# The low part of the weights, made by an adding DMA in one granule of eight of the feed-forward products

## The chip, the cores and the metric

The kernel runs on one core of a Trainium2 chip. The metric is the device time of one execution in microseconds (us): the median over the runs, before and after the change. The core has five engines that work side by side and meet at semaphores: TensorE (matmuls, PE in the profile), VectorE (DVE), ScalarE (ACT), GpSimd (POOL) and SyncE (SP, which here only issues DMAs). Data lies in SBUF, matmuls add up in PSUM, and DMAs move data between HBM and SBUF.

## The reference

One layer of a decoder trunk in float32, for 256 tokens of width 2048. Cut to what matters:

```python
h = rms_norm(x, norm_mix)
proj = h @ w_in                       # 2048 x 5400, for four mixers
...                                   # the mixers; each normed; concatenated
x = x + mixed @ w_out                 # 2048 x 2048
h = rms_norm(x, norm_ffn)
x = x + (silu(h @ w_ffn_gate) * (h @ w_ffn_up)) @ w_ffn_down
#            2048 x 5632           2048 x 5632       5632 x 2048
```

The feed-forward part, the last line, is what the change touches.

## The kernel before, in words

Every large product goes through the generator `product` (L120). It multiplies both tiles of 128 tokens by one block of 512 columns of a weight matrix, and so has two accumulators in PSUM, `a[0]` and `a[1]`. Weights and activations are split in two parts each, a rounded high part and the low part that is left, and three of the four partial products are summed: high by high (L146), high by the weights' low part (L147), low by the weights' high part (L148).

The rows of the weight matrix are taken in granules of two blocks of 128 (GRAN = 2). For each granule:

- SyncE loads 512 KB into `raw` (L134; six buffers of 128 partitions by 1024 floats),
- ScalarE copies it rounded into `wh` (L137; three buffers),
- VectorE makes `wl`, `raw` minus `wh` (L138; three buffers),
- TensorE runs 12 matmuls: two token tiles by two blocks by L146, L147, L148.

The feed-forward part (L785 to L805) runs, for each of 11 blocks of 512 hidden columns, a gate product and an up product of 8 granules each. ScalarE applies Silu to the gate's sums (L790), VectorE multiplies by the up product (L793), and `hidden_T` transposes the result and splits it into `gh` and `gl` (L777 to L782); it runs after granule 1 of the next gate product. Then come four down products of 22 granules each, one for each 512 output columns; VectorE adds the residual (L804), and SyncE and ScalarE store. That makes 11 x 8 + 11 x 8 + 4 x 22 = 264 granules.

The program is written in order, but a scheduler lays down the order of each engine's instructions when the program is built (L836, `TileContext` with a timeline simulation): it may put an instruction ahead of another one when the other's inputs or buffers are, in its model, not yet there. On the chip each engine then runs its own list in that order, and waits on semaphores for data and for buffers to come free.

Of the kernel before, what the change touches and what calls it, by code (L numbers as in the profile page):

```python
# [8 lines left out]
F32 = mybir.dt.float32  # L9
F32R = mybir.dt.float32r  # L10
BF16 = mybir.dt.bfloat16
AF = mybir.ActivationFunctionType
ALU = mybir.AluOpType
# [4 lines left out]
P = 128  # L18
T = 256
D_MODEL = 2048  # L20
KT = D_MODEL // P
# [12 lines left out]

# First distance of each relative-position bucket (distances up to T - 1).
BUCKET_STARTS = [0, 1, 2, 3, 4, 5, 6, 7, 8, 9, 10, 11, 12, 13, 14, 15, 16, 21, 27, 35, 46, 59, 77,
                 99, 128, 166, 216]

# Columns of w_in.
C_Q, C_KV, C_B, C_C, C_D = 0, 512, 1304, 2840, 3864  # L40


class Blocks:
    """A [P, KT, T] operand kept as tiles of four blocks each."""

# [9 lines left out]
def trunk(ctx: ExitStack, tc: tile.TileContext, x, w_in, w_out, norm_mix, norm_ffn, q_gain, k_gain,  # L55
# [10 lines left out]

# [1 line left out]
    nc.scalar.preload_act_table_set("natural_log_exp_and_others")  # L68
# [19 lines left out]

    # the tensor engine runs at half its clock until it has been busy for a while
    warm = misc.tile([P, GW], F32, name="ps")  # L90
# [10 lines left out]

# [1 line left out]
    def rstd(pool, ss, n, count, eps, name):  # L103
        """(ss / count + eps) ** -0.5 over [P, n]."""
        r = pool.tile([ss.shape[0], n], F32, name=name)
        nc.gpsimd.tensor_scalar(r, ss, 1.0 / count, eps, op0=ALU.mult, op1=ALU.add)
        nc.gpsimd.tensor_tensor(r, r, mhalf[:ss.shape[0], :n], op=ALU.pow)
        return r

    def split_T(hi, lo, kt, srcs, gain):  # L110
        """Transposes of two token tiles into column block kt of hi and lo, times gain."""
        p = misc.tile([P, GW], F32, name="ps")
        for t in range(2):
            nc.tensor.transpose(p[:, t * P:(t + 1) * P], srcs[t], ident)  # L114
        g = gain[:, kt:kt + 1]
        nc.scalar.activation(hi[:, kt, :], p[:, :T], AF.Copy, scale=g)  # L116
        nc.vector.scalar_tensor_tensor(lo[:, kt, :], p[:, :T], g, hi[:, kt, :].bitcast(F32),
                                       op0=ALU.mult, op1=ALU.subtract)

    def product(w, c0, n, hi, lo, nkt, order=None, before=None, mids=()):  # L120
        """[hi + lo]^T @ w[:, c0:c0 + n] for both token tiles, in three passes of 12-bit parts.

        Yields after each granule of GRAN blocks; mids[i] runs after granule i + 1."""
        a = [acc.tile([P, GW], F32, name="acc") for _ in range(2)]
        order = list(order or range(0, nkt, GRAN))
        for g, k0 in enumerate(order):
# [5 lines left out]
            for i in range(0, GRAN, step):  # L132
                ii = slice(i, i + step)
                nc.sync.dma_start(raw[:, ii, :n], wv[:, ii, :])  # L134
                if before is not None and i == 0:
                    before(k0)
                nc.scalar.activation(wh[:, ii, :n], raw[:, ii, :n], AF.Copy)  # L137
                nc.vector.tensor_tensor(wl[:, ii, :n], raw[:, ii, :n], wh[:, ii, :n].bitcast(F32),  # L138
                                        op=ALU.subtract)
# [16 lines left out]
    def residual(c, a):  # L156
        """Add a to column chunk c of x, and take its sum of squares."""
        for t in range(2):
# [5 lines left out]
    def run(gen):  # L164
        """Drive a generator to its end."""
        while True:
            try:
                next(gen)
            except StopIteration as e:
                return e.value  # L170

# [1 line left out]
    h1h = hpool.tile([P, KT, T], F32R, name="h1h", tag="hh")  # L173
# [25 lines left out]
    def slot(k, name, shape=(P, 2, GW), dtype=F32):  # L199
        """One of the eight tiles that end up holding the mixed operand."""  # L200
        return mp.tile(list(shape), dtype, name=name, tag=f"m{k}")
# [5 lines left out]
    with tc.tile_pool(name="mix", bufs=1) as mix:  # L207
# [18 lines left out]
        def group_norm(o):  # L226
            """RMSNorm, without the gain, of o [P, 2, GW] in place."""
            s = mix.tile([P, 2], F32, name="gss", bufs=2)
# [7 lines left out]
        def group_T(o, group, k):  # L236
            """o, transposed and times the gain, as a group's blocks of the mixed operand."""
            mixed(group, k)
            for kt in range(4):
                split_T(mh, ml, group * 4 + kt, [o[:, t, kt * P:(kt + 1) * P] for t in range(2)], ggain)  # L240

# [1 line left out]
        oh = mix.tile([32, 256], F32, name="oh", tag="quarter", bufs=2)  # L243
# [13 lines left out]

        # ================= group A: native sparse attention ======================================
        # ---- queries
        qs = evacuate(aq, "qs", dst=slot(2, "qs"))  # L260
# [41 lines left out]

        # ---- compressed branch
        zp = slot(1, "zp", (P, 16, 2, 2, NCMP))
# [17 lines left out]

        # ---- keys, values, gates
        w1 = [slot(4 + b, f"w1_{b}", (P, 8, 2, 64)) for b in range(2)]
# [8 lines left out]
        a = run(product(w_in, C_KV, 512, h1h, h1l, KT, mids=[None, None, None, queries_T]))  # L333
        # the compressed branch's columns twice over, for a transpose into both halves
        for t in range(2):
# [7 lines left out]

        # ---- the other products, a granule at a time between the steps of the attention
        mids, got = {}, {}
# [104 lines left out]

        # gates: wg[p, r, g, t, b] = sigmoid
        ge = mix.tile([P, 2, 24], F32, name="ge")
# [6 lines left out]

        # masks  # L460
        negf = mix.tile([P, P], F32, name="negf", tag="quarter", bufs=2)
# [21 lines left out]
        nc.gpsimd.memset(hc, 0.0)  # L483
        # gelu(h) = h / (1 + exp(-2 c (h + 0.044715 h^3)))
        h_ = mix.tile([P, 2 * NCMP], F32, name="h_")
# [12 lines left out]
        pump(1)  # L498
        # keys: kcT[(g', d), (g, n)], zero where g' != g
        p = misc.tile([P, GW], F32, name="ps")  # L500
# [15 lines left out]
        nc.scalar.activation(kcT, p[:, :32], AF.Copy, scale=gk)  # L516
        # values: vcb[(r, g, n), (r', g'), d], zero off the diagonal
        hv = mix.tile([P, 4, 32], F32, name="hv", tag="quarter", bufs=2)
# [7 lines left out]
        pump(1)  # L526
        # scores and softmax
        rv = const.tile([P, 2], F32, name="rv")
# [37 lines left out]

        # ---- selected (all blocks are) and window (all keys are in reach) branches
        mn = mix.tile([P, 4, 2, 2, 2], F32, name="mn")
# [68 lines left out]

        # ================= group D: stick-breaking attention ======================================
        od = big("od")
        zs, ss, parts, ats = {}, {}, {}, {}  # L640

        def diagonal(v):
            """Zero the query-key pairs of the diagonal blocks whose key isn't before the query."""
            v = v.rearrange("p (b c) -> p b c", c=P)[:, 0:3:2, :]
# [3 lines left out]
        def logits(h):  # L648
# [5 lines left out]
                             skip_group_check=True)  # L654
            # softplus(z) = max(z, 0) + log(1 + exp(-|z|))
            b = mix.tile([P, 384], F32, name="e", bufs=3)
# [52 lines left out]
        group_T(od, 3, 2)  # L709
        # ================= group C: causal spatial gating =========================================  # L710
        tril = const.tile([P, P], F32, name="tril")
# [30 lines left out]

        # both wait with group C's blocks until it is done
        outs = [out_product(0, [spatial]), out_product(1, [lambda: group_T(uu, 2, 6)])]
# [5 lines left out]

    # ================= output projection, residual, transposed FFN input ==========================
    h2h = hpool.tile([P, KT, T], F32R, name="h2h", tag="hh")
# [13 lines left out]
    with tc.tile_pool(name="ffn", bufs=2) as ffn:  # L766
        # ================= SwiGLU FFN =============================================================
        gh = ffn.tile([P, FKT, T], F32R, name="gh", bufs=1)
# [16 lines left out]
        for c in range(NFF):  # L785
            before_ = (lambda: input_T(3)) if c == 0 else (lambda: hidden_T(c - 1))
            a = run(product(w_gate, c * GW, GW, h2h, h2l, KT, mids=[before_]))
            s = ups[c] = ffn.tile([P, 2, GW], F32, name="s")
            for t in range(2):
                nc.scalar.activation(s[:, t, :], a[t], AF.Silu, scale=rs2[:, t:t + 1])  # L790
            a = run(product(w_up, c * GW, GW, h2h, h2l, KT))
            for t in range(2):
# [3 lines left out]
        for c in range(4):  # L796
            a = run(product(w_down, c * GW, GW, gh, gl, FKT,
                            mids=[lambda: hidden_T(NFF - 1)] if c == 0 else ()))
# [41 lines left out]
```

## Time and profile before

| | |
|---|---|
| median of 2 runs | 1142.0 us (1141.68 to 1142.32) |
| span of the profiled execution | 1141.3 us |
| TensorE busy, share of the span | 99% |
| VectorE busy | 51% |
| ScalarE busy | 46% |
| GpSimd busy | 5% |
| moved by DMA | 208.85 MB, mean 183 GB/s |

The profile is of one execution, taken by the hardware profiler. Its span runs from the first to the last instruction and here lies 0.7 us below the median of the timed runs. Its views: a page with the busy time of each engine, the chain of work that ended last (followed back from the last instruction to what released it, step by step), the costliest groups of instructions and the DMA issues; the waits, by who waited for whom; the timeline of single instructions; and tables of busy time by stretch, with the clock granted to TensorE (1.00 is full) and the busy share of the 16 DMA engines. In these views L and a number is a line of the kernel, `out<-in` names the tiles, and PEld is TensorE's weight load, which runs beside the matmuls. Matmuls overlap each other: one shows 0.39 us, but the next starts earlier.

### The profile page before, as it was taken

How to read it: one execution, taken by the hardware profiler on the slowest of the kernel's cores; microseconds unless marked ns; L12 is line 12 of the kernel's file. 1: busy time of each engine (PE TensorE's matmuls, PEld its weight loads, DVE VectorE, ACT ScalarE, POOL GpSimd, SP SyncE). 2: the span in 40 equal slices, each digit the busy share in tenths (PEclk: the TensorE clock that was granted, in tenths of full speed). 3: DMA queues.
4: the chain of work that ended last, by engine and by line, in shares of the span. 5: the costliest groups of instructions: out<-in, count | busy, mean ns of one | idle time of the engine just before them, and what ended most of it. 6: DMA issues, size and time to landing. Idle time of an engine off the chain costs nothing.

```text
span 1141.3 us, 13742 instructions
## 1 busy us (share of the span) xinstructions
PE 1131.6 (99%) x5275; PEld 935.9 (82%) x5275; DVE 587.0 (51%) x697; ACT 520.2 (46%) x669; POOL 54.2 (5%) x96
## 2 busy tenths in 40 slices
PE   8999999999999999999999999999999999999998
PEld 6898777888888888888888888888888888888887
DVE  5565444556566554454454554544544544444443
ACT  6454455555545544444444444444444434343432
POOL 3210001222000000000000000000000000000000
PEclk9999999999999999999999999999999999999999
DMA  9774433545555566666666666666666567666761
GB/s 279 250 259 146 146 112 111 152 144 148 165 171 177 178 190 190 186 188 196 186 186 198 187 189 189 190 190 186 189 195 186 186 197 209 199 206 197 204 199 62
DMA packets 115186, 208.85 MB, mean 183 GB/s; under 512 B 11204, under 2 KB 18464, under 8 KB 114992
## 3 DMA queue, kind: packets, MB, share of 16 engines
q1 hardware_dynamic: 113168, 204.21, 60.5%
q0 software_dynamic: 800, 2.71, 0.7%
q10 hardware_dynamic: 1152, 1.05, 0.3%
q8 instruction: 41, 0.67, 0.2%
q14 instruction: 25, 0.20, 0.1%
HBM read 205.84 MB, written 3.68 MB: 184 GB/s over the span
## 4 chain that ended last, share of the span: by engine, by line
PE 98%; DMA 1%; DVE 0%; SPq 0%; ACT 0%; issue 0%; DVEq 0%
PE acc L147 30%; PE acc L148 30%; PE acc L146 30%; PE ps L777 1%; PE ps L114 1%; DMA xs<-in_x 1%; PE ps L580 1%; PE ps L592 1%; PE ps L579 1%; PE ps L652 0%; PE ps L605 0%; PE ps L480 0%; PE ps L603 0%; DVE zp L317 0%; PE ps L604 0%; PE ps L653 0%
## 5 line engine op out<-in xcount | busy, mean ns | idle before, releaser
L138 DVE TENSOR_TENSOR wl<-raw,wh 128x1024 fp32r<-128x1024 f32 (+2 forms) x385 | 466.9, 1213 | 493.5 <-ACT wh L137 493.3
L137 ACT ACTIVATE wh<-raw 128x1024 fp32r<-128x1024 f32 (+2 forms) x385 | 404.1, 1050 | 535.1 <-PE acc L148 506.3
L148 PE MATMUL acc<-wh,h2l 128*128 128x512 f32 x704 | 274.0, 389 | 0.0
L147 PE MATMUL acc<-wl,h2h 128*128 128x512 f32 x704 | 273.9, 389 | 0.0
L146 PE MATMUL acc<-wh,h2h 128*128 128x512 f32 x704 | 249.9, 390 | 0.0
L148 PEld LDWEIGHTS acc<-wh,h2l 128*128 128x128 f32 x704 | 132.1, 188 | 27.6
L147 PEld LDWEIGHTS acc<-wl,h2h 128*128 128x128 f32 x704 | 132.2, 188 | 27.1
L146 PEld LDWEIGHTS acc<-wh,h2h 128*128 128x128 f32 x704 | 132.2, 188 | 27.1
L148 PE MATMUL acc<-wh,gl 128*128 128x512 f32 x352 | 137.0, 389 | 0.0
L147 PE MATMUL acc<-wl,gh 128*128 128x512 f32 x352 | 136.9, 389 | 0.0
L147 PE MATMUL acc<-wl,h1h 128*128 128x512 f32 (+1 forms) x352 | 136.4, 388 | 0.4 <-DVE wl L138 0.4
L146 PE MATMUL acc<-wh,h1h 128*128 128x512 f32 (+1 forms) x352 | 132.7, 391 | 1.7 <-ACT h1h L116 1.7
L148 PE MATMUL acc<-wh,h1l 128*128 128x512 f32 (+1 forms) x352 | 134.2, 388 | 0.0
L146 PE MATMUL acc<-wh,gh 128*128 128x512 f32 x352 | 123.1, 389 | 0.0
L146 PEld LDWEIGHTS acc<-wh,h1h 128*128 128x128 f32 x352 | 66.1, 189 | 14.7 <-ACT h1h L116 2.0
L147 PEld LDWEIGHTS acc<-wl,h1h 128*128 128x128 f32 x352 | 66.5, 189 | 13.4 <-issue 1.0
L146 PEld LDWEIGHTS acc<-wh,gh 128*128 128x128 f32 x352 | 66.0, 188 | 13.8
L147 PEld LDWEIGHTS acc<-wl,gh 128*128 128x128 f32 x352 | 66.1, 188 | 13.7
L148 PEld LDWEIGHTS acc<-wh,gl 128*128 128x128 f32 x352 | 66.1, 188 | 13.7
L148 PEld LDWEIGHTS acc<-wh,h1l 128*128 128x128 f32 x352 | 66.0, 189 | 12.3 <-DVE wl L138 0.4
L147 PE MATMUL acc<-wl,mh 128*128 128x512 f32 x128 | 50.1, 393 | 0.0
L148 PE MATMUL acc<-wh,ml 128*128 128x512 f32 x128 | 49.4, 391 | 0.0
(259 smaller groups left out, 654.2 us busy)
## 6 DMA issues: line engine op xcount, KB each, us to landing
raw<-in_w_ffn_gate SPq DMA_DIRECT2D x88, 512.0 KB, 4.4
raw<-in_w_ffn_up SPq DMA_DIRECT2D x88, 512.0 KB, 3.7
raw<-in_w_ffn_down SPq DMA_DIRECT2D x88, 512.0 KB, 4.5
raw<-in_w_in SPq DMA_DIRECT2D x79, 512.0 KB, 3.6
raw<-in_w_out SPq DMA_DIRECT2D x32, 512.0 KB, 3.9
raw<-in_w_in SPq DMA_DIRECT2D x8, 280.0 KB, 3.7
xs<-in_x SPq DMA_DIRECT2D x8, 256.0 KB, 8.2
cdr<-cdr POOLq DMA_DIRECT2D x1, 1536.0 KB, 9.2
```

The source lines that it names most:

```text
L114: nc.tensor.transpose(p[:, t * P:(t + 1) * P], srcs[t], ident)
L137: nc.scalar.activation(wh[:, ii, :n], raw[:, ii, :n], AF.Copy)
L138: nc.vector.tensor_tensor(wl[:, ii, :n], raw[:, ii, :n], wh[:, ii, :n].bitcast(F32), op=ALU.subtract)
L146: nc.tensor.matmul(a[t][:, :n], h, wh[:, i, :n], start=first, stop=False)
L147: nc.tensor.matmul(a[t][:, :n], h, wl[:, i, :n], start=False, stop=False)
L148: nc.tensor.matmul(a[t][:, :n], l, wh[:, i, :n], start=False, stop=last)
L579: nc.tensor.matmul(s[:, 0:128], q_[:, 0:128], k_[:, 0:128], start=True, stop=True)
L580: nc.tensor.matmul(s[:, 128:384], q_[:, 128:256], k_, start=True, stop=True)
L592: nc.tensor.transpose(p[:, c * P:(c + 1) * P], es[u][:, c * P:(c + 1) * P], ident)
L777: nc.tensor.transpose(p[:, i * T + t * P:i * T + (t + 1) * P], ups[c][:, t, (2 * k + i) * P:(2 * k + i + 1) * P], ident)
```

## The change

`product` gets a list, `dma_low`, of granules whose low part is made in another way. In such a granule ScalarE writes minus the rounded `raw` into `wl` (a second copy, with scale -1), and a DMA issued from GpSimd adds `raw` onto `wl` in SBUF; VectorE's subtract is left out. Gate and up products name granule 5 (of 0 to 7), the down products granules 5 and 13 (of 0 to 21).

```diff
-    def product(w, c0, n, hi, lo, nkt, order=None, before=None, mids=()):
+    def product(w, c0, n, hi, lo, nkt, order=None, before=None, mids=(), dma_low=()):
...
                 nc.scalar.activation(wh[:, ii, :n], raw[:, ii, :n], AF.Copy)
+                if g in dma_low:
+                    nc.scalar.activation(wl[:, ii, :n], raw[:, ii, :n], AF.Copy, scale=-1.0)
+                    nc.gpsimd.dma_start(wl[:, ii, :n].bitcast(F32), raw[:, ii, :n], accum_op=ALU.add)
+                    continue
                 nc.vector.tensor_tensor(wl[:, ii, :n], raw[:, ii, :n], wh[:, ii, :n].bitcast(F32),
                                         op=ALU.subtract)
...
-            a = run(product(w_gate, c * GW, GW, h2h, h2l, KT, mids=[before_]))
+            a = run(product(w_gate, c * GW, GW, h2h, h2l, KT, mids=[before_], dma_low=(5,)))
...
-            a = run(product(w_up, c * GW, GW, h2h, h2l, KT))
+            a = run(product(w_up, c * GW, GW, h2h, h2l, KT, dma_low=(5,)))
...
-            a = run(product(w_down, c * GW, GW, gh, gl, FKT,
+            a = run(product(w_down, c * GW, GW, gh, gl, FKT, dma_low=(5, 13),
                             mids=[lambda: hidden_T(NFF - 1)] if c == 0 else ()))
```

The rest of the diff takes comments out.

## Rows read from the trace of the kernel before

**Rows 1.** The page: busy time of each engine; the chain that ended last.

```profile
PE 1131.6 (99%) x5275; PEld 935.9 (82%) x5275; DVE 587.0 (51%) x697; ACT 520.2 (46%) x669; POOL 54.2 (5%) x96
...
PE 98%; DMA 1%; DVE 0%; SPq 0%; ACT 0%; issue 0%; DVEq 0%
```

**Rows 2.** TensorE's waits, first and last of five: us, times, longest.

```profile
PE ps L93 <- POOL ident masks.py:199: 2.6, 1, 2.6
...
PE acc L147 <- DVE wl L138: 0.4, 1, 0.4
```

**Rows 3.** The page's groups: busy us, mean ns, idle before, what ended it.

```profile
L138 DVE TENSOR_TENSOR wl<-raw,wh 128x1024 fp32r<-128x1024 f32 (+2 forms) x385 | 466.9, 1213 | 493.5 <-ACT wh L137 493.3
L137 ACT ACTIVATE wh<-raw 128x1024 fp32r<-128x1024 f32 (+2 forms) x385 | 404.1, 1050 | 535.1 <-PE acc L148 506.3
```

**Rows 4.** Timeline, 702.5 to 709 us: start, us, engine, instruction, idle before.

```profile
702.55 0.39 PE L147 MATMUL acc<-wl,h2h 128*128 128x512 f32 x1
702.78 0.39 PE L148 MATMUL acc<-wh,h2l 128*128 128x512 f32 x1
...
703.00 0.62 PE L146 MATMUL acc<-wh,h2h 128*128 128x512 f32 x2
703.20 1.06 ACT L137 ACTIVATE wh<-raw 128x1024 fp32r<-128x1024 f32 x1 [1.66 <-PE acc L148]
...
704.30 1.23 DVE L138 TENSOR_TENSOR wl<-raw,wh 128x1024 fp32r<-128x1024 f32 x1 [1.50 <-ACT wh L137]
...
708.44 0.62 PE L146 MATMUL acc<-wh,h2h 128*128 128x512 f32 x2
...
708.90 0.39 PE L147 MATMUL acc<-wl,h2h 128*128 128x512 f32 x1
```

**Rows 5.** Stretches of 510 to 1141: length, busy by engine, clock, DMA share, GB/s.

```profile
700.00:850.00 150.00, 150.00 (x675) 124.40 (x675) 74.41 (x67) 64.01 (x66) 0.00 (x0) 1.00 0.65 190
...
sum 631.00, PE 627.49 PEld 519.91 DVE 305.20 ACT 259.10 POOL 0.00; mean PE 125.50 PEld 103.98 DVE 61.04 ACT 51.82 POOL 0.00
```

**Rows 6.** Timeline of GpSimd: the issue of its 1024 KB DMA.

```profile
54.98 0.92 POOL L255 DMA_DIRECT2D tb<-cdr  x1 [8.86 <-DMA cdr<-cdr]
```

**Rows 7.** DMA issues: count, KB each, median us from issue to landing.

```profile
raw<-in_w_ffn_gate SPq DMA_DIRECT2D x88, 512.0 KB, 4.4
...
cdr<-cdr POOLq DMA_DIRECT2D x1, 1536.0 KB, 9.2
...
tb<-cdr POOLq DMA_DIRECT2D x1, 1024.0 KB, 6.7
...
cdr<-csb POOLq DMA_DIRECT2D x1, 12.0 KB, 2.6
```

**Rows 8.** The stretch of 2 us with the highest rate, 44 to 64 us.

```profile
58.00:60.00 2.00, 2.00 (x13) 1.77 (x13) 0.11 (x1) 1.67 (x4) 0.00 (x0) 1.00 1.06 392
```

**Rows 9.** Timeline of TensorE behind the pair of L146 at 703.00.

```profile
703.91 0.39 PE L146 MATMUL acc<-wh,h2h 128*128 128x512 f32 x1
704.14 0.39 PE L147 MATMUL acc<-wl,h2h 128*128 128x512 f32 x1
704.36 0.39 PE L148 MATMUL acc<-wh,h2l 128*128 128x512 f32 x1
704.59 0.39 PE L147 MATMUL acc<-wl,h2h 128*128 128x512 f32 x1
```

**Rows 10.** DMA queues: packets, MB, share of 16 engines' span; the loads' queue.

```profile
q1 hardware_dynamic: 113168, 204.21, 60.5%
```

**Rows 11.** Timeline of TensorE from 6 us; stretches of 1 us, 9 to 13 us.

```profile
8.16 0.50 PE L146 MATMUL acc<-wh,h1h 128*128 128x512 f32 x1 [1.74 <-ACT h1h L116]
...
9.93 0.47 PE L114 MATMUL ps<-ident,xs 128*128 128x128 f32 x1 [0.56 <-DMA xs<-in_x]
...
9.00:10.00 1.00, 0.44 (x3) 0.07 (x2) 0.44 (x1) 0.89 (x2) 1.00 (x6) 0.71 1.08 353
10.00:11.00 1.00, 1.00 (x5) 1.00 (x6) 1.00 (x2) 0.00 (x0) 1.00 (x2) 0.50 1.08 374
...
12.00:13.00 1.00, 1.00 (x4) 0.77 (x4) 0.39 (x1) 1.00 (x3) 0.00 (x0) 0.58 1.10 361
```

## The prediction

> **What bounds the kernel now.** I read the page first. TensorE is busy for 99% of the span, VectorE for 51%, ScalarE for 46%, GpSimd for 5%, and the chain that ended last runs through TensorE for 98% of the span [rows 1]. So the reader is to see one full engine and three with room. TensorE's waits of over 0.15 us are five in the whole run, the longest 2.6 us at the start and the shortest 0.4 us, and none of their lines belongs to the feed-forward part alone [rows 2]. VectorE's subtract (L138) is busy for 466.9 us, but VectorE has been idle for 493.5 us ahead of its instances; of ScalarE's rounding copy (L137) it is 404.1 and 535.1, mostly until TensorE gives a buffer back [rows 3]. Taking work from VectorE can therefore gain nothing: no matmul of this stage waits for it.
>
> Next the timeline of the middle of a gate product, for how far ahead the parts are made [rows 4]. A granule is 12 matmuls and begins with a pair of L146; from 703.00 to 708.44 there are two of them, so one takes 2.72 us, 12 x 0.227 us, without a gap. With three `wh` and three `wl`, the end of a granule frees buffers for the one three later: the copy that starts at 703.20 makes `wh` for the granule of 708.44. It ends at 704.26, the subtract runs from 704.30 to 705.53, and the first matmul that reads this `wl` (L147) is due at 708.90. The low part is ready 3.37 us early. That cover is all that the change can spend.
>
> **The change, part by part.** It touches granule 5 of each gate and up product, 11 + 11, and granules 5 and 13 of the four down products, 8: 30 granules of 264.
>
> *Removed:* 30 subtracts of 1.23 us, 37 us of VectorE. Worth nothing on the path, by the 3.37 us above.
>
> *Added on ScalarE:* 30 copies with scale -1, of the form of L137, 1.06 us each, 32 us. Ahead of an L137 ScalarE has been idle for 1.66 us [rows 4], and no Silu or transposed hidden block stands at these granules, so the copy doesn't delay the next `wh`. But the DMA must wait for it. In the program's order (`wh` first) it runs from 704.26 to 705.32, and GpSimd can issue at about 705.36, with the 0.04 us that VectorE needs behind ScalarE.
>
> *Added on GpSimd's queue:* 30 DMAs of 512 KB from SBUF to SBUF that add onto their destination. GpSimd does nothing in the stage [rows 5], so nothing is queued behind them. The largest issue took GpSimd 0.92 us [rows 6]; that lies within the landing times below. No row shows an accumulating DMA, nor one between SBUF tiles, so its landing is bounded by the plain ones of that queue: 12 KB took 2.6 us, 1024 KB 6.7 us, 1536 KB 9.2 us from issue to landing [rows 7], all beside weight loads.
> - Lower end: the fixed 2.6 us, and 512 KB at the best rate of a 2 us stretch, 392 GB/s [rows 8], 1.3 us: 3.9 us. As a plain copy between the 12 KB and the 1024 KB row: 2.6 + 500/1012 x 4.1 = 4.6 us.
> - Middle: an add has to read the source and the old destination, 1024 KB in: the 1024 KB row, 6.7 us.
> - Upper end: two reads and the write in turn, 1536 KB: 9.2 us.
>
> I take 6.7 us, because the second read can't be left out, while the write can run beside reads, as it did in the copies of those rows. The Trainium skill (Collectives: The Full Stack, "Why ReduceScatter is half of AllGather") says that the add in a DMA costs nothing by itself but needs two source reads on one read queue, and so halves the rate; by that the middle is right, and no run here shows it yet. The Trainium skill's fit for a DMA from this queue (DMA: Bandwidth & Descriptors, "Anatomy of one DMA") is 2.0 us plus the bytes at 436 GB/s; an estimate by it is 3.2 us for 512 KB and would leave no stall, but the same fit gives 4.4 us for the 1024 KB that took 6.7 us here, so the row decides.
>
> *The stall.* 705.36 + 6.7 = 712.06 against 708.90: 3.16 us. Can TensorE do something else meanwhile? In the order of this run the L147 at 704.59 has no L146 just ahead of it: that L146 is the second of the pair at 703.00, the first one of the other accumulator, taken ahead. Within one accumulator the order L146, L147, L148 is kept [rows 9]. So after two matmuls both accumulators stand before an L147, and the next product can't start, because its `wh` needs a buffer of the granules in between. Nothing fills the gap, and nothing gives it back, since TensorE has no idle time later. What is late next is nothing: the two granules behind have their parts ready by then, and the following copies again run two granules ahead. So 30 x 3.16 = 95 us. The profiled span of 1141.3 us lies 0.7 us below the median of 1142.0, so I add to the median: 1142 + 95 = **1237 us**.
>
> *Loads.* `raw` is held until the DMA lands, 712.06 in place of 705.53, and the load of the granule six later waits for it, with SP's later loads queued behind. That load's `wh` starts 5.24 us before its granule of 708.44 + 6 x 2.72 = 724.76, at 719.52: 14.0 us after 705.53, of which the load takes 4.4 [rows 7]. Of the 9.6 us left 6.5 go, while the granule itself moves by 3.2. Hidden; without this cover each us would come on top 30 times. The loads' queue takes 0.605 of 1141.3 us for 204.21 MB [rows 10], 1.77 us per 512 KB; two passes are 3.5 us in a product of 8 granules, 21.8 us, so that the share of 0.65 [rows 5] becomes about 0.8. That is not full.
>
> **The rivals.**
> 1. *The clock falls too, or the landing is long.* Between 6.4 and 9.9 us TensorE stood still for 1.74 us, ran four matmuls, stood for another 0.56 us, and the granted clock went to the lower level: 0.71, 0.50, 0.50, 0.58 of full in the four us from 9 to 13 [rows 11]. That lost 0.29 + 0.50 + 0.50 + 0.42 = 1.7 us. A stall of 3.2 us is longer than those two together, but has full work on both sides. If each of the 30 brings it, 51 us: 1288 us. If the landing takes 9.2 us, the stall is 5.66 us and the time 1312 us, with the clock 1363 us. For it: nothing in the rows excludes it. Against: in the feed-forward stage the clock has been 1.00 throughout [rows 5], but with no stall to test it.
> 2. *The stall is smaller.* The minus copy needs only `raw` and a `wl`, and the last reader of a `wl` (702.55 + 0.39 = 702.94) ends before the last of the `wh` (703.17). The order on each engine is laid down at build by a scheduler that moves instructions, as the L146 shows. If it puts the minus copy first, ScalarE ends it at 704.03, the issue is at 704.07, and 6.7 us leave 1.87 us: 56 us, 1198 us. Against: the program has `wh` first. A plain copy's 4.6 us in the program's order leaves 1.06 us, 32 us, 1174 us.
> 3. *Hidden: not slower.* The cover decides. With the minus copy first the DMA has 4.83 us, and a landing of 4.6 or 3.9 us fits: 1142 us. In the program's order it has 3.54 us, and 3.9 us leaves 0.36 us, 11 us in all, 1153 us, within 2%. Both need an add that costs no more than a plain copy. The Trainium skill's fit named above would make it so, and the 1024 KB row disagrees with it. A time below 1142 us has no mechanism, since 12 x 0.227 us per granule stay: a small chance only.
> 4. *It doesn't do what it says:* other matmuls might fill the stall. The three buffers exclude that, as said; it is counted under 3.
>
> **How the numbers follow.** Forecast (a stall of about 2 to 4 us in the program's order, the clock held): 0.42, its own range 1200 to 1265 us. Rival 1: 0.28, above 1265 us, up to 1363. Rival 2: 0.15, 1165 to 1200 us. Rivals 3 and 4: 0.13 within 2%, 1142 to 1165 us, and 0.02 faster. Under 2% (23 us) is about what a measurement of this kernel can't tell from no change. So faster 0.02, same 0.13, slower 0.42 + 0.28 + 0.15 = 0.85. The range leaves out rival 3 and the very longest landings: 1160 to 1360 us.
>
> **What would show each step.** In the profile of the changed kernel: 355 subtracts in place of 385; a new group of 30 copies of 1.06 us; 30 DMAs of 512 KB from GpSimd, whose median landing I expect at 6.7 us; a wait of TensorE, at the matmul that reads `wl`, for that DMA, 30 times and about 3.2 us each, 95 us in all, where there was none; a chain that ended last with some 8% of DMA and less TensorE. The order of the two copies on ScalarE tells rival 2, the granted clock behind each stall rival 1. The prediction is wrong if the landing is under 3.5 us or over 9.2 us, or if TensorE has other work in the stall.

## The result and the profile after

The changed kernel takes 1168.54 us in the median of two runs (1167.38 to 1169.69) against 1142.0 us: a ratio of 1.023, with a 95% interval of 1.0213 to 1.0247. It is slower, in the direction forecast, but by 26.5 us and not by 95 us. The profiled execution has a span of 1167.7 us, 26.4 us more than before, so the profile holds the whole of the loss.

The page of the changed kernel: busy time, the chain that ended last by engine, and the groups that answer to [rows 1] and [rows 3] (busy us, mean ns, idle before, what ended it). The numbers of lines are now five higher.

```profile
PE 1139.8 (98%) x5275; PEld 933.6 (80%) x5275; DVE 549.8 (47%) x667; ACT 548.6 (47%) x699; POOL 80.3 (7%) x126
...
PE 79%; DMA 13%; issue 3%; ACT 2%; DVE 1%; SPq 0%; DVEq 0%; POOLq 0%; ACTq 0%
...
L143 DVE TENSOR_TENSOR wl<-raw,wh 128x1024 fp32r<-128x1024 f32 (+2 forms) x355 | 429.7, 1211 | 556.0 <-ACT wh L138 554.2
...
L141 POOL DMA_DIRECT2D wl<-raw x30 | 26.0, 865 | 696.7 <-ACT wl L140 580.9
L140 ACT ACTIVATE wl<-raw 128x1024 fp32r<-128x1024 f32 x30 | 31.8, 1061 | 41.5 <-PE acc L152 41.5
...
wl<-raw POOLq DMA_DIRECT2D x30, 512.0 KB, 5.4
```

The parts are those that the diff says: 30 subtracts fewer, 30 copies of 1.06 us and 30 DMAs of 512 KB more, with a median landing of 5.4 us. VectorE has given up 37 us and nothing came of it. Two entries differ from what was expected: the landing, 5.4 in place of 6.7 us, and what ended ScalarE's idle time ahead of the minus copy. That is TensorE's L152, the last reader of a `wl`, and not the copy into `wh`.

TensorE's waits (us in total, times, longest) answer to [rows 2]:

```profile
PEld acc L152 <- DMA wl<-raw: 30.3, 30, 1.9
...
PE acc L152 <- DMA wl<-raw: 17.8, 21, 1.5
```

The first row counts from when the weight load could have run, the second only the idle time after the running matmul has ended; the loss lies between them. Counted from the timeline, as the time between when a first L152 was due and when it started, the 30 stalls sum to 22.5 us, 0.75 us in the mean, from 0.00 to 1.61 us; the matmul after a stall also takes 0.34 us to the next in place of 0.227, some 3 us more in all. That leaves about 1 us of the 26.4 us unexplained. One stall in the timeline, in the first down product (TensorE's other matmuls left out):

```profile
1007.02 1.06 ACT L140 ACTIVATE wl<-raw 128x1024 fp32r<-128x1024 f32 x1 [1.43 <-PE acc L152]
...
1007.98 1.04 ACT L138 ACTIVATE wh<-raw 128x1024 fp32r<-128x1024 f32 x1
...
1008.37 0.86 POOL L141 DMA_DIRECT2D wl<-raw  x1 [21.67 <-ACT wl L140]
...
1012.48 0.61 PE L151 MATMUL acc<-wh,gh 128*128 128x512 f32 x2
...
1014.07 0.19 PEld L152 LDWEIGHTS acc<-wl,gh 128*128 128x128 f32 x1 [1.40 <-DMA wl<-raw]
1014.07 0.50 PE L152 MATMUL acc<-wl,gh 128*128 128x512 f32 x1 [0.97 <-DMA wl<-raw]
...
1014.41 0.40 PE L153 MATMUL acc<-wh,gl 128*128 128x512 f32 x1
```

The minus copy (L140) comes first, the copy into `wh` (L138) after it. GpSimd issues 0.29 us behind the end of the copy (1008.08 to 1008.37). The pair of L151 starts at 1012.48, so L152 was due 2 x 0.227 us later, at 1012.94, and ran at 1014.07: 1.13 us late, 5.7 us after the issue. The weight load (PEld) of that L152 waits for the DMA too and starts together with the matmul, where elsewhere it runs ahead; that would explain the 0.34 us, but no run separates it. This is rival 2 of the prediction, with a shorter landing than it used.

### The profile page after: what moved, and what is told of

Its sections match the earlier page's. It is cut to its first block, busy times and chain, and to the rows that moved or that the text cites. A ratio compares the mean times of both kernels' runs of the same rounds, so it can differ in the third digit from the quotient of the medians.

```text
span 1167.7 us, 13830 instructions
## 1 busy us (share of the span) xinstructions
PE 1139.8 (98%) x5275; PEld 933.6 (80%) x5275; DVE 549.8 (47%) x667; ACT 548.6 (47%) x699; POOL 80.3 (7%) x126
## 4 chain that ended last, share of the span: by engine, by line
PE 79%; DMA 13%; issue 3%; ACT 2%; DVE 1%; SPq 0%; DVEq 0%; POOLq 0%; ACTq 0%
PE acc L152 25%; PE acc L153 24%; PE acc L151 23%; DMA wl<-raw 11%; ACT wl L140 2%; DMA raw<-in_w_ffn_down 1%; PE ps L114 1%; PE ps L782 1%; DVE wl L143 1%; ACT wh L138 1%; PE ps L585 1%; PE ps L597 1%; DMA xs<-in_x 1%; PE ps L584 1%; DMA raw<-in_w_ffn_gate 0%
## 5 line engine op out<-in xcount | busy, mean ns | idle before, releaser
L143 DVE TENSOR_TENSOR wl<-raw,wh 128x1024 fp32r<-128x1024 f32 (+2 forms) x355 | 429.7, 1211 | 556.0 <-ACT wh L138 554.2
L138 ACT ACTIVATE wh<-raw 128x1024 fp32r<-128x1024 f32 (+2 forms) x385 | 403.4, 1048 | 490.7 <-PE acc L153 470.5
L152 PE MATMUL acc<-wl,h2h 128*128 128x512 f32 x704 | 276.5, 393 | 10.4 <-DMA wl<-raw 9.9
L153 PE MATMUL acc<-wh,h2l 128*128 128x512 f32 x704 | 274.3, 390 | 0.0
L151 PE MATMUL acc<-wh,h2h 128*128 128x512 f32 x704 | 250.0, 391 | 0.0
L152 PEld LDWEIGHTS acc<-wl,h2h 128*128 128x128 f32 x704 | 132.2, 188 | 45.6 <-DMA wl<-raw 19.0
L151 PEld LDWEIGHTS acc<-wh,h2h 128*128 128x128 f32 x704 | 132.2, 188 | 27.2
L153 PEld LDWEIGHTS acc<-wh,h2l 128*128 128x128 f32 x704 | 132.2, 188 | 26.9
L152 PE MATMUL acc<-wl,gh 128*128 128x512 f32 x352 | 137.9, 392 | 7.9 <-DMA wl<-raw 7.9
L153 PE MATMUL acc<-wh,gl 128*128 128x512 f32 x352 | 137.0, 389 | 0.0
L152 PE MATMUL acc<-wl,h1h 128*128 128x512 f32 (+1 forms) x352 | 136.3, 388 | 0.4 <-DVE wl L143 0.4
L153 PE MATMUL acc<-wh,h1l 128*128 128x512 f32 (+1 forms) x352 | 134.2, 388 | 0.0
L151 PE MATMUL acc<-wh,h1h 128*128 128x512 f32 (+1 forms) x352 | 132.6, 391 | 1.5 <-ACT h1h L116 1.5
L151 PE MATMUL acc<-wh,gh 128*128 128x512 f32 x352 | 123.0, 389 | 0.0
L152 PEld LDWEIGHTS acc<-wl,gh 128*128 128x128 f32 x352 | 66.1, 188 | 24.8 <-DMA wl<-raw 11.3
L151 PEld LDWEIGHTS acc<-wh,h1h 128*128 128x128 f32 x352 | 66.1, 189 | 14.4 <-ACT h1h L116 1.8
L152 PEld LDWEIGHTS acc<-wl,h1h 128*128 128x128 f32 x352 | 66.5, 189 | 13.4 <-issue 1.0
L151 PEld LDWEIGHTS acc<-wh,gh 128*128 128x128 f32 x352 | 66.1, 188 | 13.7
L153 PEld LDWEIGHTS acc<-wh,gl 128*128 128x128 f32 x352 | 66.1, 188 | 13.5
L153 PEld LDWEIGHTS acc<-wh,h1l 128*128 128x128 f32 x352 | 66.0, 189 | 12.3 <-DVE wl L143 0.4
L141 POOL DMA_DIRECT2D wl<-raw x30 | 26.0, 865 | 696.7 <-ACT wl L140 580.9
L140 ACT ACTIVATE wl<-raw 128x1024 fp32r<-128x1024 f32 x30 | 31.8, 1061 | 41.5 <-PE acc L152 41.5
```

The source lines that it names most:

```text
L140: nc.scalar.activation(wl[:, ii, :n], raw[:, ii, :n], AF.Copy, scale=-1.0)
L141: nc.gpsimd.dma_start(wl[:, ii, :n].bitcast(F32), raw[:, ii, :n], accum_op=ALU.add)
L151: nc.tensor.matmul(a[t][:, :n], h, wh[:, i, :n], start=first, stop=False)
L152: nc.tensor.matmul(a[t][:, :n], h, wl[:, i, :n], start=False, stop=False)
L153: nc.tensor.matmul(a[t][:, :n], l, wh[:, i, :n], start=False, stop=last)
```

## The experiments

**What is to be told apart.** Theory: each stall is the DMA's landing less its cover, the time from the issue to the first L152; the cover is set by the `wl` buffer that comes free and by which copy ScalarE makes first, and the landing by the second read of the add and by the weight loads beside it. Rivals: the order of the copies is of no account; ScalarE's second copy is itself what costs; the DMA costs through the loads that it delays; the landing is fixed cost, and the add is free.

**The order of the two copies.** The minus copy is made to depend on `wh`:

```diff
-                    nc.scalar.activation(wl[:, ii, :n], raw[:, ii, :n], AF.Copy, scale=-1.0)
+                    nc.scalar.activation(wl[:, ii, :n], wh[:, ii, :n].bitcast(F32), AF.Copy, scale=-1.0)
```

> The minus copy reads wh instead of raw (the same values), so that ScalarE has to make wh first, as the program is written. Theory (the stall is the DMA's landing less the cover, and the cover is set by which copy comes first): the issue moves back by the 0.97 us from one copy's start to the next, each of the 30 stalls grows by about as much, 29 us in all, from 1168.5 to about 1197 us. Rival (the order of the copies is of no account, because something else, such as the DMA engines' load, ends the wait): 1165 to 1172 us. If stalls of some 2 us made the clock fall, over 1220 us.

Measured: 1196.03 us, ratio 1.0473 (1.0457 to 1.0488). The timeline of one granule:

```profile
513.49 1.06 ACT L138 ACTIVATE wh<-raw 128x1024 fp32r<-128x1024 f32 x1 [1.58 <-PE acc L153]
514.58 1.06 ACT L140 ACTIVATE wl<-wh 128x1024 fp32r<-128x1024 f32 x1
515.93 0.85 POOL L141 DMA_DIRECT2D wl<-raw  x1 [23.57 <-ACT wl L140]
...
518.73 0.61 PE L151 MATMUL acc<-wh,h2h 128*128 128x512 f32 x2
520.77 0.50 PE L152 MATMUL acc<-wl,h2h 128*128 128x512 f32 x1 [1.43 <-DMA wl<-raw]
```

The minus copy starts 1.09 us after the copy into `wh`, as the prediction had it, and the stall here is 520.77 - 518.73 - 0.45 = 1.59 us; 28 of the 30 lie between 1.5 and 1.7 us. So forcing the order costs 1196.0 - 1168.5 = 27.5 us, near the 29 us of the theory, but by two errors that offset each other: the issue moved back by 1.3 us (3.25 us ahead of when L152 is due, in place of 4.57) and not by 0.97 us, while the landing, 4.8 us in the median, is 0.6 us shorter than in the changed kernel, which the theory didn't have. The longest stall is 2.6 us, and the clock granted in the 2 us stretches around it stayed at 1.00:

```profile
1079.07 0.50 PE L152 MATMUL acc<-wl,gh 128*128 128x512 f32 x1 [2.44 <-DMA wl<-raw]
```

```profile
1080.00:1082.00 2.00, 2.00 (x11) 1.64 (x10) 0.00 (x0) 0.28 (x1) 0.00 (x0) 1.00 0.77 195
```

**A buffer of its own for the low part.** In the 30 granules `wl` comes from the feed-forward part's pool, one buffer:

```diff
-            wl = wpool.tile([P, GRAN, GW], F32R, name="wl")
+            if g in dma_low:
+                wl = low_pool.tile([P, GRAN, GW], F32R, name="wd", bufs=1)
+            else:
+                wl = wpool.tile([P, GRAN, GW], F32R, name="wl")
...
```

> The low part of the 30 granules gets a buffer of its own, apart from the three wl, so that the minus copy needs no release by the granule three before. Theory (the cover is short only because the wl buffer comes free 5.5 us before the first matmul that reads it): the copy and the DMA run a granule or more earlier, no stall is left, 1142 to 1145 us. Rival (the DMA costs through the DMA engines or the held raw buffer, by delaying weight loads): still over 1155 us, with TensorE or ScalarE waiting for raw.

Measured: 1143.19 us, ratio 1.0007 (0.9998 to 1.0016). TensorE has no wait for the DMA left; in one granule the minus copy waits only for `raw` and starts 16.6 us before the L155 that reads its `wd`:

```profile
494.97 1.06 ACT L143 ACTIVATE wd<-raw 128x1024 fp32r<-128x1024 f32 x1 [2.32 <-DMA raw<-in_w_ffn_gate]
...
511.55 0.39 PE L155 MATMUL acc<-wd,h2h 128*128 128x512 f32 x1
```

The same 30 DMAs, with landings of 4.7 to 6.8 us, now cost nothing that can be measured. So the loss is the short cover, and not the DMA engines' load. This run says nothing of the held `raw`: all 30 DMAs land before the copy into `wh` of the same granule starts (here at 501.12 and 508.80 us), and that copy holds `raw` as long as before. The changed kernel does: there `raw` is held until the landing, and its waits show none of TensorE or of a ScalarE copy for a load in the feed-forward part.

**The add itself.** A plain copy in place of the adding one:

```diff
-                    nc.gpsimd.dma_start(wl[:, ii, :n].bitcast(F32), raw[:, ii, :n], accum_op=ALU.add)
+                    nc.gpsimd.dma_start(wl[:, ii, :n].bitcast(F32), raw[:, ii, :n])
```

> The DMA copies raw onto wl without adding; the low part of these granules is therefore wrong (it holds the whole weight). All else is as in the changed kernel, the order of the copies too. Theory (the add costs a second read, so that 512 KB move at 197 GB/s where a plain load reaches 390): the transfer takes 1.3 to 1.5 us less, landing at about 4 us in place of 5.4, within the cover: 1142 to 1148 us. Rival (the landing is fixed cost and waiting behind the weight loads, the add is free): landing stays over 5 us, 1163 to 1170 us.

Measured: 1147.91 us, ratio 1.0047 (1.003 to 1.0063), with ScalarE's order as in the changed kernel. Landings, shortest, median and longest, in the changed kernel and here:

```profile
DMA to landing us min/median/max: 4.5/5.4/6.1
```

```profile
DMA to landing us min/median/max: 2.9/4.0/5.3
```

The add costs 1.6 us on the shortest landing and 1.4 us on the median; without it, 20.6 of the 26.5 us are gone. How long the DMA engines are taken by it stands in the pages, in the row of GpSimd's queue (packets, MB, share of 16 engines' span): before, in the changed kernel, and here.

```profile
q0 software_dynamic: 800, 2.71, 0.7%
```

```profile
q0 software_dynamic: 5120, 18.44, 7.8%
```

```profile
q0 software_dynamic: 5120, 18.44, 4.2%
```

Less the 8 us of before (0.7% of 1141.3), 30 DMAs take 83 us with the add and 40 us without: 2.8 and 1.3 us each for the same 512 KB written. The add takes the engines twice as long. That this is the second read is the reading that fits; the rows count what is written and show no read.

**VectorE in place of the DMA.** The minus copy stays:

```diff
-                    nc.gpsimd.dma_start(wl[:, ii, :n].bitcast(F32), raw[:, ii, :n], accum_op=ALU.add)
+                    nc.vector.tensor_tensor(wl[:, ii, :n], raw[:, ii, :n], wl[:, ii, :n].bitcast(F32), op=ALU.add)
```

> The minus copy stays on ScalarE, and VectorE adds raw onto it in place of the DMA. Theory (ScalarE has room, and only the DMA's landing costs): 1142 us, as before, no wait of TensorE. Rival (the extra copy of 1.06 us delays the next wh or its matmuls): up to 30 x 1.06 = 32 us more, 1160 to 1174 us.

Measured: 1142.6 us, ratio 0.9999 (0.999 to 1.0008), no wait of TensorE in the feed-forward part. ScalarE's extra copy is hidden.

**Fewer loads beside the DMA.** In the feed-forward products three of four granules use the `raw` of the one before:

```diff
-            raw = wpool.tile([P, GRAN, GW], F32, name="raw", bufs=6)
+            fresh = not dma_low or g % 4 == 0
+            if fresh:
+                raw = wpool.tile([P, GRAN, GW], F32, name="raw", bufs=6)
...
-                nc.sync.dma_start(raw[:, ii, :n], wv[:, ii, :])
+                if fresh:
+                    nc.sync.dma_start(raw[:, ii, :n], wv[:, ii, :])
```

> In the feed-forward part only every fourth granule is loaded, and the three after it use the same raw (so the products there use wrong weights); the minus copy, the DMA and all matmuls stay. Theory (the landing runs from 4.5 to 6.1 us because weight loads share the DMA engines with it): all landings come near the lowest, 4.5 us, and the stalls sum to under 6 us: 1143 to 1149 us. Rival (the spread comes from GpSimd's issue or from VectorE beside it): landings stay at 5.4 us in the median, 1163 to 1170 us.

> The same quarter of the loads, but the low part made by VectorE in every granule, as before the change: what fewer loads do to the time without the DMA (the products of the feed-forward part use wrong weights). Both theories: 1141 to 1142 us, since TensorE never waits for loads in the feed-forward part.

Measured: 1148.51 us with the DMA, ratio 1.0052 (1.0037 to 1.0067), and 1143.13 us with VectorE's subtract in its place, 1.0005 (0.9995 to 1.0015). So the loads themselves are worth nothing, and with a quarter of them the DMA costs 5.4 us, 0.18 us a granule: a landing of 4.5 us just about equals the cover (1012.94 - 1008.37 = 4.57 us in the stall shown above). Of the 5.4 us only 1.3 us are lateness; 3.1 us are the first matmul behind each wait, which takes 0.29 to 0.34 us to the next here too, though 28 of the 30 are late by 0.1 us at most. Landings, and stretches of 1 us behind an issue at 597.45 us (the last two columns are the share of the DMA engines and GB/s):

```profile
DMA to landing us min/median/max: 4.5/4.5/5.2
```

```profile
598.00:599.00 1.00, 1.00 (x6) 0.84 (x5) 0.00 (x0) 0.11 (x1) 0.31 (x1) 1.00 0.30 57
599.00:600.00 1.00, 1.00 (x7) 0.81 (x6) 0.00 (x0) 0.96 (x1) 0.00 (x0) 1.00 1.04 201
600.00:601.00 1.00, 1.00 (x6) 0.84 (x5) 0.86 (x1) 0.10 (x1) 0.00 (x0) 1.00 1.07 201
601.00:602.00 1.00, 1.00 (x6) 0.66 (x5) 0.36 (x1) 0.24 (x1) 0.00 (x0) 1.00 0.36 66
```

Without loads beside it the add fills the DMA engines for about 2.8 us (0.30 + 1.04 + 1.07 + 0.36), at up to 201 GB/s. In the changed kernel the same stretch, behind the issue at 1008.37 us, carries loads as well:

```profile
1009.00:1010.00 1.00, 1.00 (x7) 0.81 (x6) 0.00 (x0) 0.06 (x2) 0.23 (x1) 1.00 0.82 272
1010.00:1011.00 1.00, 1.00 (x6) 0.84 (x5) 0.00 (x0) 1.00 (x1) 0.00 (x0) 1.00 1.03 260
1011.00:1012.00 1.00, 1.00 (x6) 0.84 (x5) 0.94 (x1) 0.02 (x1) 0.00 (x0) 1.00 1.07 209
1012.00:1013.00 1.00, 1.00 (x5) 0.56 (x3) 0.28 (x1) 0.32 (x1) 0.00 (x0) 1.00 0.69 131
```

What is above 201 GB/s are loads, and the add ends about a us later for them. The spread of 4.5 to 6.1 us is nearly all the loads': with a quarter of them 28 of the 30 landings lie between 4.5 and 4.6 us. It also shows by product: the 11 granules of the gate products stall by 0.00 to 0.37 us, the 11 of the up products by 0.55 to 1.36 us. Whether the gate's eight transposes shift the loads out of the DMA's way was not tried.

**Two halves.** Minus copy and DMA for each block of 128 rows by itself:

```diff
-                    nc.scalar.activation(wl[:, ii, :n], raw[:, ii, :n], AF.Copy, scale=-1.0)
-                    nc.gpsimd.dma_start(wl[:, ii, :n].bitcast(F32), raw[:, ii, :n], accum_op=ALU.add)
+                    for j in range(i, i + step):
+                        jj = slice(j, j + 1)
+                        nc.scalar.activation(wl[:, jj, :n], raw[:, jj, :n], AF.Copy, scale=-1.0)
+                        nc.gpsimd.dma_start(wl[:, jj, :n].bitcast(F32), raw[:, jj, :n], accum_op=ALU.add)
```

> The minus copy and the DMA of a granule are done in two halves, one for each block of 128 rows. Theory (TensorE needs the first block's low part first and the second's three matmuls, 0.68 us, later; the first half can be issued after half a copy, and moves half the bytes): the stall falls from about 0.85 us to 0.1 to 0.4 us, 1145 to 1155 us. Rival (the fixed part of a DMA, 1.4 us from issue to the first packet, and two issues of 0.86 us in turn on GpSimd outweigh it): 1163 to 1180 us.

Measured: 1147.77 us, ratio 1.0044 (1.0029 to 1.0059). The 60 DMAs of 256 KB land in 4.7 us in the median: the first halves in 4.2 us, the second ones, issued 0.5 to 0.7 us later while the first is under way, in 5.0 us. The first half is issued some 0.45 us sooner than the whole was, and TensorE needs the second 0.68 us later. TensorE's waits for `wl` shrink to two of 2.5 us together. The time lies in the theory's range; how much of the gain is the earlier issue and how much the shorter first landing was not separated.

The longer of the two waits, in a down product, shows something that the theory didn't ask for. The pair of L153 ahead of it started at 1033.17, so TensorE was 2.3 us late (landing 7.2 us), and the clock, 1.00 until then, fell to its lower level right behind the stall:

```profile
1035.90 0.50 PE L154 MATMUL acc<-wl,gh 128*128 128x512 f32 x1 [2.11 <-DMA wl<-raw]
```

```profile
1036.00:1038.00 2.00, 2.00 (x7) 1.58 (x8) 0.00 (x0) 0.00 (x0) 0.00 (x0) 0.68 0.02 4
1038.00:1040.00 2.00, 2.00 (x6) 1.61 (x5) 0.00 (x0) 0.05 (x1) 0.00 (x0) 0.50 0.72 166
1040.00:1042.00 2.00, 2.00 (x10) 1.57 (x9) 0.96 (x1) 1.01 (x1) 0.00 (x0) 0.97 1.01 385
```

That lost 0.64 + 1.00 + 0.06 = 1.7 us on top of the stall. A stall of 2.6 us in the run with the order forced did not do it. So the length of a stall alone does not settle whether the clock falls.

**A longer stall, for the clock.** The DMA is issued twice, the second waiting for the first:

```diff
-                    nc.scalar.activation(wl[:, ii, :n], raw[:, ii, :n], AF.Copy, scale=-1.0)
+                    nc.scalar.activation(wl[:, ii, :n], raw[:, ii, :n], AF.Copy, scale=-2.0)
                     nc.gpsimd.dma_start(wl[:, ii, :n].bitcast(F32), raw[:, ii, :n], accum_op=ALU.add)
+                    nc.gpsimd.dma_start(wl[:, ii, :n].bitcast(F32), raw[:, ii, :n], accum_op=ALU.add)
```

> The minus copy has scale -2 and the DMA is issued twice, the second after the first has landed (so the low part of these granules is twice what it should be). The stall grows by one landing, 5.4 us, to about 6.3 us. Theory (a stall costs its own length): 30 x 5.4 = 162 us more than the changed kernel, about 1331 us. Rival (a stall this long also brings TensorE's clock down, for the 1.7 us that the start of the run lost by it): 1.7 us more at each, about 1380 us, with the granted clock under 1.00 behind the stalls.

Measured: 1395.43 us, ratio 1.2217 (1.2199 to 1.2235): the rival, and a little over it. One stall, and the stretches of 2 us around it (the column ahead of the last two is the granted clock):

```profile
551.12 0.80 PE L153 MATMUL acc<-wl,h2h 128*128 128x512 f32 x1 [5.54 <-DMA wl<-raw]
551.71 0.63 PE L154 MATMUL acc<-wh,h2l 128*128 128x512 f32 x1
```

```profile
546.00:548.00 2.00, 0.00 (x0) 0.00 (x0) 1.22 (x1) 0.22 (x1) 0.49 (x1) 1.00 0.88 271
548.00:550.00 2.00, 0.00 (x0) 0.00 (x0) 0.00 (x0) 0.00 (x0) 0.00 (x0) 0.83 1.08 210
550.00:552.00 2.00, 0.88 (x2) 0.79 (x3) 0.00 (x0) 0.00 (x0) 0.00 (x0) 0.50 0.16 29
...
554.00:556.00 2.00, 2.00 (x7) 1.54 (x6) 0.00 (x0) 0.15 (x1) 0.00 (x0) 0.50 0.79 303
556.00:558.00 2.00, 2.00 (x10) 1.65 (x9) 1.06 (x1) 0.90 (x1) 0.00 (x0) 0.96 0.01 5
```

Its pair of L152 started at 544.96, so TensorE is late by 551.12 - 545.42 = 5.7 us. With TensorE idle, the clock goes from 2.4 GHz to its lower level, 1.2 GHz, before 550 us, and is back up by about 556 us, behind some 5 us of matmuls without a gap. The 11 matmuls from 551.12 to 555.98 us take 4.9 us in place of 2.5: 2.4 us on top of the stall. Together 8.1 us; the whole run lost (1394.4 - 1141.3) / 30 = 8.4 us at each granule.

## Why the prediction was wrong

The prediction had the right mechanism and the right place, and failed in two of its terms: the order of ScalarE's copies, and the landing, which was the larger one. It put the stall at 3.16 us; it measured 0.75 us in the mean.

- **What bounds the kernel, and that VectorE's time is worth nothing:** right. With the 37 us of subtracts gone and no stall the time is 1143.2 us.
- **The place of the loss, TensorE at the matmul that reads `wl`, 30 times, after two matmuls, with nothing to fill the gap:** right. The pair of L151 ahead of each stall and no other work in it show it.
- **ScalarE's copies in the program's order: the first step that failed.** The scheduler put the minus copy first. Rival 2 had the mechanism, a `wl` free before a `wh`, and the 1.3 us earlier issue, at 0.15 with a small stall as its neighbour. The evidence was at hand: a list order in which TensorE's L146 is taken ahead of earlier matmuls means that the program's order is no argument. It was worth 27.5 us, shown by forcing the other order (net of the landing that is shorter there).
- **The landing of 6.7 us: the second step, a term mis-sized.** It is 5.4 us beside the loads, 4.8 us when issued a us later, and 4.5 us without loads. The principle held: an add takes the DMA engines twice as long as a plain copy, 2.8 against 1.3 us. The size did not: the 1024 KB row from HBM [rows 7] took 4.1 us over the 12 KB row, while an add of 512 KB between SBUF tiles moves in 2.8 us, and the part that is fixed was 4.5 - 2.8 = 1.7 us in place of 2.6 us. The packets in the trace of before show where the 6.7 us of the 1024 KB row went: they took the engines 2.9 us, about as long as the add's, but the first began 2.4 us behind the issue (the adds' mostly 1.4 us) and 0.29 MB of other queues went through the engines among them. So the bytes were priced rightly, and what the row had besides them was carried over with them; why its first packet came a us later stays open. In the program's order the time was 1196 us and not 1237 us. The term itself is 30 x (6.7 - 4.8) = 57 us; some 12 us that the prediction left out (the next point but one, and the slower matmul behind a stall) went the other way.
- **The Trainium skill's two rules, taken together, would have been nearer.** The rule on two source reads (Collectives: The Full Stack, "Why ReduceScatter is half of AllGather") agrees with 201 GB/s written at full DMA engines, where a load reached 392 [rows 8], and with 2.8 against 1.3 us of the engines. The fit of "Anatomy of one DMA" (DMA: Bandwidth & Descriptors) gives 3.2 us for 512 KB, near the plain copy's shortest 2.9 us, and for the 1024 KB that the add reads an estimate of 4.4 us, near the measured 4.5 us. I had set that fit aside because of one row.
- **GpSimd behind ScalarE:** 0.29 us, not the 0.04 us that VectorE shows; 0.25 us each, 7.5 us in all, towards the prediction.
- **The sum, mended:** 704.03 + 0.29 + 5.27, the mean landing, = 709.59 against 708.90, and 0.04 us to the matmul: 0.73 us, 30 times 22 us, and some 3 us of slower restarts: 1167 us by 1168.5 measured. With the measured terms and the measured order the prediction's own formula gives the result, and in the other order, with its landing of 4.8 us, 705.35 + 0.29 + 4.8 + 0.04 - 708.90 = 1.58 us, 47 us and again some 3 us: 1193 us by 1196 us measured.
- **The clock:** held, as forecast, but over stalls of 1.6 us at most and not over the 3.2 us for which the prediction argued it. Rival 1 was nearer than it looked: among the other runs a stall of 2.6 us left the clock alone, one of 2.3 us brought it down once, with full work on both sides, and those of 5.6 us and more brought it down each time. What 30 stalls of 3.2 us would have done stays open.
- **Loads and `raw`:** right, hidden: in the changed kernel `raw` is held until the DMA lands, and no wait of TensorE for a load came of it.

## What to carry to other kernels

Where a full engine waits for a part that is made ahead, the cost of a slower way to make it is its latency less the cover, at each place; price both from rows, ask what else ran on the DMA engines in the row that a landing is taken from, and where a scheduler lays down the order, work out which instruction's buffer comes free first instead of trusting the program's order. An adding DMA between SBUF tiles is worth considering only where its destination is free long before its use: with a buffer of its own it cost nothing here, and with the shared three it cost 0.9 us each. Taking time from an engine that nobody waits for gained nothing here, whoever took it over.

## What the runs showed of the hardware

An add of 512 KB from SBUF to SBUF issued from GpSimd landed in 4.5 us with hardly any load beside it, a plain copy in 2.9 us at its shortest; the add moved 201 GB/s with the DMA engines full and took them 2.8 us, the plain copy 1.3 us. Two halves of 256 KB, one behind the other, landed in 4.2 and 5.0 us in the median. A stall of TensorE of 5.7 us cost 2.4 us more, nearly all of it at the lower clock; one of 2.3 us brought the clock down too and cost 1.7 us more, while one of 2.6 us left it at full. The first matmul behind a wait for the DMA took 0.34 us to the next, in place of 0.227, even where it was not late.
